# The border between two layers of a one-core trunk: norm loads, last scatter, first key projection and row sums in another order

## The chip, the cores and the metric

The kernel runs on one core of a Trainium2 chip. The time is that of one execution on the device, in microseconds (us). Next to it stands one profiled execution, whose span is somewhat shorter than its time. PE is the matrix engine, PEld its weight load, DVE the vector engine, ACT the scalar engine, POOL the general engine. SP is a queue of its own that only issues DMA transfers here, and POOL issues some too. PEclk is the clock that the matrix engine was granted, as a share of the full one.

## The reference, cut to what matters

Two layers are run one after the other on 512 tokens of width 1024. Each has three parts, and after each part stands a layer norm.

```
for l in range(DEPTH):                                   # DEPTH = 2
    q, k, v, r, a_low, u, v_sgu = split_proj(x @ w_in[l])
    h = concat([gla_group(...), sgu_group(...)]) @ w_out[l]
    x = layer_norm(DN_ALPHA * x + h, ln_g[l, 0], ln_b[l, 0])
    h = mem_xattn(x, mem, wq_x[l], wk_x[l], wv_x[l], wo_x[l])   # keys: mem @ wk_x[l]
    x = layer_norm(DN_ALPHA * x + h, ln_g[l, 1], ln_b[l, 1])
    h = grouped_moe(x, ...)                              # 16 experts, two for each token
    x = layer_norm(DN_ALPHA * x + h, ln_g[l, 2], ln_b[l, 2])
```

The border is the end of the experts of layer 0, the third layer norm of layer 0, the keys of layer 1, which hang on `mem` alone, and the first token projection of layer 1, which needs the normed x.

## The kernel before, in words

Each product of two fp32 matrices is made of three fp16 products: both operands are split into a high and a low half (`mm3`, L168 to L170: high by high, high by low, low by high). The four tiles of 128 tokens are called 0 to 3, and `xr[t]` holds the residual of tile t.

Weights come in units of 1 MB. `feed.fill` (L98) issues their loads on SP as slots come free. `feed.pump` (L124 and L129) splits the next unit that has been loaded: ACT makes `whi` from `raw`, then DVE makes `wlo` from both. `feed.limit` bounds how far the loads may run ahead of the layer. The units of layer 1 begin with wk0 to wk3 (the keys), then k, v0, v1, s0 (the token projections).

The order of the instructions on each engine is the order of the code. Each engine works its own list in order, so an instruction that waits holds up all that stand behind it on that engine.

At the end of the experts, `down(e)` multiplies by the last weight of an expert, ACT writes the result into `rows` (L1234), and POOL issues an indirect scatter of these rows into a table `y` in memory (L1143). `down(14)` is called in the loop, `down(15)` after it. Then every engine reads a counter `cnti` (L1260) and takes a branch (L1261) around an overflow loop, which isn't entered with these inputs. After it the third layer norm, class `LN3`, reads two rows of `y` for each token, `ya` (L399) and `yb` (L400), in tile order on SP's queue. `ya + yb` is made by DVE for tile 0 (L409) and by POOL for tiles 1 to 3 (L405). `a(t)` adds the residual (DVE L412) and takes the variance (ACT L415 to L417). `b(t)` scales by `lng` and `lnb` (DVE L422 and L423).

Around it stands the first stage of layer 1: four `k_proj`, each 48 matmuls on a wk unit and a split of the result into `kT` (ACT L173, DVE L174); `xTr(t)`, eight PE transposes of the normed tile (L310), evicted as `xT` by the same two lines; and `tok_proj(t)`, the first products of layer 1 on `xT`. `warm(10)` (L185) is ten matmuls whose result nobody reads. Much later in layer 1 the output projection splits its own weight units with the same lines L124 and L129.

Of the kernel before, what the change touches and what calls it, by code (L numbers as in the profile page):

```python
# [11 lines left out]
F32 = mybir.dt.float32  # L12
I32 = mybir.dt.int32
AF = mybir.ActivationFunctionType
OP = mybir.AluOpType
# [5 lines left out]
DEPTH = 2  # L21
D = 1024
S = 512
NT = 4
P = 128
KT = 8
NE = 16
# [11 lines left out]
YEND = 4  # L39
# [5 lines left out]
def trunk_kernel(ctx, tc, units, xT, x, memT, alow, wa2, b_a, gn_g, w_sT, b_s, slnT,  # L45
# [12 lines left out]
    def nm(s):  # L58
        cnt[0] += 1
        return f"{s}_{cnt[0]}"  # L60
# [167 lines left out]
    U = []  # L228
# [117 lines left out]
    def kv_open():  # L346
        KV["cm"] = tc.tile_pool(name=nm("kv"), bufs=1, reuse_waits="tile")
        kp = KV["cm"].__enter__()
        KV["k"] = [kp.tile([P, KT, 256], F16, name=nm("kT")) for _ in range(2)]
# [44 lines left out]
    class LN3:  # L394
        def __init__(self, ya, yb):
            ln_exp()
            self.ya, self.yb, self.st = ya, yb, {}
            for t in range(NT):
                nc.sync.dma_start(ya[:, t], y2[t * P:(t + 1) * P, :])  # L399
                nc.sync.dma_start(yb[:, t], y2[S + t * P:S + (t + 1) * P, :])  # L400
                if t == 1:
                    feed.limit = 1 << 30
                    feed.fill()
            for t in range(1, NT):
                pool.tensor_tensor(ya[:, t], ya[:, t], yb[:, t], op=OP.add)  # L405

        def a(self, t):
            if t == 0:
                dve.tensor_tensor(self.ya[:, 0], self.ya[:, 0], self.yb[:, 0], op=OP.add)  # L409
            pre = xr[t]  # L410
            mv_ = lnp[0].tile([P, 6], F32, tag="lnmv", bufs=2, name=nm("lnmv"))
            dve.scalar_tensor_tensor(pre, xr[t], ALPHA, self.ya[:, t], op0=OP.mult, op1=OP.add,  # L412
                                     accum_out=mv_[:, 0:1])
            dve.tensor_scalar(mv_[:, 1:2], mv_[:, 0:1], -1.0 / D, None, op0=OP.mult)
            act.activation(self.yb[:, t], pre, AF.Square, bias=mv_[:, 1:2], accum_out=mv_[:, 2:3])  # L415
            act.activation(mv_[:, 3:4], mv_[:, 2:3], AF.Ln, bias=c_lneps, scale=1.0 / D)
            act.activation(mv_[:, 4:5], mv_[:, 3:4], AF.Exp, scale=-0.5)  # L417
            self.st[t] = pre, mv_

        def b(self, t):  # L420
            pre, mv_ = self.st.pop(t)
            dve.scalar_tensor_tensor(pre, pre, mv_[:, 1:2], lgt["g"], op0=OP.add, op1=OP.mult)  # L422
            dve.scalar_tensor_tensor(xr[t], pre, mv_[:, 4:5], lgt["b"], op0=OP.mult, op1=OP.add)  # L423

    kv_open()
    ln_open()
    for l in range(DEPTH):
        u = U[l]

        with ExitStack() as ex:  # L430
# [25 lines left out]
            if l > 0:  # L456
                k_proj(u, 0)
                third.a(0)
                k_proj(u, 1, 0)
                third.a(1)  # L460
                third.b(0)
                feed.pump(1)
                k_proj(u, 2, 0)
                k_proj(u, 3, 0)
                xTr(0)
                feed.pump(2)
            kg = mp.tile([P, 2, NT, 256], F32, tag="kgu", name="kg")
# [28 lines left out]
            for t in range(NT):  # L496
                if t == NT - 1:
# [3 lines left out]
                    act.activation(al[:, :, 1, 0:16], araw, AF.Copy, scale=SW)  # L501
                if l > 0 and t + 1 < NT:
                    if t + 2 < NT:
                        third.a(t + 2)
                    third.b(t + 1)
                if l > 0 and t == 1:
                    warm(10)
                p = pk[t] if l == 0 else tok_proj(t, [u["k"]], 256)
# [360 lines left out]
        with ExitStack() as ex:  # L869
# [6 lines left out]
            feed.xend = {"h": u["end"], "x": u["end"] - (8 if fin else 0), "y": u["end"] - (8 if fin else YEND), "mem": u["end"]}  # L876
            feed.limit = u["end"] + 4
            feed.rawfree.extend("x" * RAW_X)
# [327 lines left out]

            def down_mm(e, after=None):
                hh, hl = E[e]["hT"]
                pp = []
                for hf in range(2):  # L1210
# [8 lines left out]
                    else:  # L1219
                        feed.pump()  # L1220
                        wh, wl = feed.get(n)
# [7 lines left out]

            def down(e, after=None):  # L1230
                o = rows[:, 2 + e % 2]
                pp = down_mm(e, after)
                for hf in range(2):
                    act.activation(o[:CAP, hf * 512:(hf + 1) * 512], pp[hf][:CAP, :], AF.Copy,  # L1234
                                   scale=(gallw if whole(e, 4 + hf) else gall)[:CAP, e:e + 1])
                scatter(o, idxR[:CAP, e:e + 1])
                del E[e]
# [91 lines left out]
            for e in range(NE - 1 if fin else NE):  # L1329
                gate_up(e)  # L1330
                if e + 1 < NE:
                    dispatch(e + 1)
                hid(e)

# [16 lines left out]

            feed.need(u["end"] - YEND - 1)
            px2c.__exit__(None, None, None)
            if not fin:
                ln_open()
                load_ln(l, 2)
                down(NE - 1)
                pxc.__exit__(None, None, None)
                phc.__exit__(None, None, None)
                with tc.tile_pool(name=f"ovf{l}", bufs=1, reuse_waits="tile") as fp:  # L1360
                    overflow(fp)
            else:

                pxc.__exit__(None, None, None)
                ln_open()
# [100 lines left out]

        if l + 1 < DEPTH:
            kv_open()


# [59 lines left out]
```

## Time and profile before

| | |
|---|---|
| median of 3 runs | 1277.48 us (1275.62 to 1279.99) |
| profiled execution | 1278.14 us, its span 1276.5 us |
| granted clock over the span | 0.972 |
| busy share of the span | PE 92%, DVE 71%, ACT 56%, POOL 18% |

Times in the rows are counted from the start of the span. "Idle before" is the time for which the engine stood still ahead of an instruction, and the name behind the arrow is what ended it. The border lies at about 610 to 690 us.

### The profile page before, as it was taken

Reading aid. Unit: us, or ns where it says so; the run is one execution under the profiler, and the core shown is the slowest. Engines: PE = TensorE matmul, PEld = TensorE weight load, DVE = VectorE, ACT = ScalarE, POOL = GpSimd, SP = SyncE. Lnnn points to the kernel's source line nnn. Section 1 sums busy time; section 2 is a strip of 40 time slices with the busy share of each in tenths; the row PEclk is TensorE's granted clock in tenths of the full one; section 3 lists DMA queues with packets and bytes.
Section 4 is the critical chain, followed back from the end, with each engine's and each line's share of the span. In section 5 each row is a group of like instructions: output and inputs, shape, how many; then the busy total and the mean of one; then the engine's idle time right before and its main releaser. Section 6 shows DMA issues by size and latency. Waiting matters only on the chain. (4 is left out here: it accounts for less than half of the span.)

```text
span 1276.5 us, 26079 instructions
## 1 busy us (share of the span) xinstructions
PE 1172.9 (92%) x11218; PEld 760.2 (60%) x11219; DVE 909.9 (71%) x1066; ACT 711.1 (56%) x810; POOL 234.5 (18%) x193
## 2 busy tenths in 40 slices
PE   7999999999979999999859999999999899999973
PEld 4455456454557777777635545444644777777751
DVE  3255875378579999999474275673857789999977
ACT  3435334345448888888443444232633588888863
POOL 3002000000231223321250003000003222223214
PEclk9999999999989999999979999999998899999996
DMA  9412225227569999999671230154374799999964
GB/s 361 163 67 99 99 77 188 99 99 292 220 226 371 419 418 418 419 417 405 233 273 79 99 133 34 67 215 181 112 312 139 274 389 419 417 419 419 373 241 180
DMA packets 54941, 314.76 MB, mean 247 GB/s; under 512 B 9310, under 2 KB 9406, under 8 KB 22561
## 3 DMA queue, kind: packets, MB, share of 16 engines
q1 hardware_dynamic: 42096, 279.99, 56.0%
q0 software_dynamic: 11568, 28.83, 6.3%
q10 hardware_dynamic: 1152, 4.19, 0.8%
q8 instruction: 90, 1.47, 0.5%
q14 instruction: 35, 0.28, 0.1%
HBM read 302.80 MB, written 22.68 MB: 255 GB/s over the span
## 5 line engine op out<-in xcount | busy, mean ns | idle before, releaser
L129 DVE SCALAR_TENSOR_TENSOR wlo<-raw,whi 128x2048 f16<-128x2048 f32 (+1 forms) x234 | 521.8, 2277 | 101.0 <-ACT whi L124 100.6
L124 ACT ACTIVATE whi<-raw 128x2048 f16<-128x2048 f32 (+1 forms) x239 | 440.9, 1894 | 32.9 <-DMA raw<-in_units 16.7
L170 PE MATMUL ps<-xgh,wlo 128*128 128x96 f16 x2048 | 270.4, 207 | 12.9 <-DVE wlo L129 12.9
L168 PE MATMUL ps<-xgh,whi 128*128 128x96 f16 x2048 | 270.3, 207 | 4.7 <-ACTq L1261 4.2
L169 PE MATMUL ps<-xgl,whi 128*128 128x96 f16 x2048 | 270.2, 207 | 1.1 <-DVE xgl L174 1.1
L170 PEld LDWEIGHTS <-wlo 128*128 128x128 f16 x2400 | 236.4, 98 | 50.7 <-DVE wlo L129 16.7
L168 PEld LDWEIGHTS <-whi 128*128 128x128 f16 x2400 | 236.5, 99 | 39.1 <-issue 6.0
L169 PEld LDWEIGHTS <-whi 128*128 128x128 f16 x2400 | 236.4, 99 | 38.2 <-issue 8.5
L1143 POOL DMA_INDIRECT y<-rows,idxR x31 | 71.4, 2303 | 340.8 <-ACT rows L1234 331.1
L168 PE MATMUL ps<-whi,xT 128*128 128x512 f16 (+1 forms) x256 | 92.6, 362 | 8.4 <-ACT whi L124 7.1
L170 PE MATMUL ps<-whi,xT 128*128 128x512 f16 (+1 forms) x256 | 92.4, 361 | 2.2 <-DVE xT L174 2.2
L169 PE MATMUL ps<-wlo,xT 128*128 128x512 f16 (+1 forms) x256 | 92.5, 361 | 1.7 <-DVE wlo L129 1.7
L168 PE MATMUL ps<-whi,hhl 128*96 128x512 f16 x200 | 75.9, 379 | 1.1 <-ACT hhl L1203 1.1
L169 PE MATMUL ps<-wlo,hhl 128*96 128x512 f16 x200 | 75.7, 379 | 0.9 <-DVE wlo L129 0.9
L170 PE MATMUL ps<-whi,hhl 128*96 128x512 f16 x200 | 75.8, 379 | 0.0
L294 ACT ACTIVATE lnmv<-lnmv,c_lneps 128x1 f32<-128x1 f32 x16 | 4.7, 295 | 110.0 <-DVE lnmv L293 110.0
L1203 ACT ACTIVATE hhl<-h 128x384 f16<-128x384 f32 x32 | 16.7, 523 | 74.9 <-DVE h L1178 74.8
L1216 PE MATMUL ps<-raw,h 128*96 128x512 f32 x112 | 50.3, 592 | 0.0
L169 PE MATMUL ps<-x2T,whi 128*128 128x512 f16 x128 | 48.5, 379 | 1.0 <-DVE x2T L174 1.0
L169 PE MATMUL ps<-wlo,mx 128*128 128x512 f16 x128 | 48.5, 379 | 0.4 <-DVE wlo L129 0.3
L1137 POOL DMA_INDIRECT rows<-xd,idxT x22 | 40.4, 1838 | 45.6 <-DVE wlo L129 11.1
L168 PE MATMUL ps<-x2T,whi 128*128 128x512 f16 x128 | 48.5, 379 | 0.0
(309 smaller groups left out, 2052.2 us busy)
## 6 DMA issues: line engine op xcount, KB each, us to landing
raw<-in_units SPq DMA_DIRECT2D x249, 1024.0 KB
xd<-xr ACTq DMA_DIRECT2D x8, 512.0 KB
ya<-y SPq DMA_DIRECT2D x8, 512.0 KB
yb<-y SPq DMA_DIRECT2D x8, 512.0 KB
y<-zr SPq DMA_DIRECT2D x1, 4096.0 KB
lng<-in_ln_g POOLq DMA_DIRECT2D x6, 512.0 KB, 5.3
lnb<-in_ln_b POOLq DMA_DIRECT2D x6, 512.0 KB, 7.1
raw<-in_xT SPq DMA_DIRECT2D x4, 512.0 KB
```

The source lines that it names most:

```text
L124: act.activation(dest[0], t[:, :cols], AF.Copy, scale=scale)
L129: dve.scalar_tensor_tensor(dest[1], t[:, :cols], scale, dest[0], op0=OP.mult, op1=OP.subtract)
L168: pe.matmul(o, lh, rh, start=first, stop=False)
L169: pe.matmul(o, lh, rl, start=False, stop=False)
L170: pe.matmul(o, ll, rh, start=False, stop=last)
L294: act.activation(mvt[:, 2:3], mvt[:, 1:2], AF.Ln, bias=c_lneps, scale=(ISC * ISC if scaled else 1.0))
L1137: pool.indirect_dma_start(out=dst[:idx.shape[0], :], out_offset=None, in_=xd[:], in_offset=bass.IndirectOffsetOnAxis(ap=idx, axis=0), boun ...
L1143: i = pool.indirect_dma_start(out=y2[:], out_offset=bass.IndirectOffsetOnAxis(ap=idx, axis=0), in_=src[:CAP, :], in_offset=None, bounds_ch ...
L1203: act.activation(f2(hh), h32, AF.Copy)
L1216: pe.matmul(p[:CAP, :], E[e]["h"][:, f * CAP:(f + 1) * CAP], mv(w, f), start=(f == 0), stop=(f == 3))
```

## The change

The norm parameters `lng` and `lnb` of the third norm are loaded while the last expert is still in work, and stand in POOL's queue ahead of the last two scatters. `down(15)` splits no weights, so that ACT writes the rows of expert 15 right behind those of expert 14, and the splits of wk2 and wk3 come after. The keys' first projection stands ahead of the branch. One more unit (k) may be loaded ahead. POOL adds no rows any more: DVE makes all four sums, tile by tile, and POOL only copies one element of `yb[:, 1]`, which keeps the instructions behind it in its list until that tile has landed. The splits, projections and norm steps of the border are written in another order, with one split fewer ahead of `tok_proj(0)` and without `warm(10)`.

```diff
     def kv_open():
-        KV["cm"] = tc.tile_pool(name=nm("kv"), bufs=1, reuse_waits="tile")
+        KV["cm"] = tc.tile_pool(name=nm("kv"), bufs=1, side="right", reuse_waits="tile")
...
-            for t in range(1, NT):
-                pool.tensor_tensor(ya[:, t], ya[:, t], yb[:, t], op=OP.add)
+
+            w = lnp[0].tile([P, 1], F32, tag="lnst", bufs=2, name=nm("lnst"))
+            pool.tensor_copy(w, yb[:, 1, 0:1])
+
+        def add(self, t):
+            dve.tensor_tensor(self.ya[:, t], self.ya[:, t], self.yb[:, t], op=OP.add)
 
         def a(self, t):
-            if t == 0:
-                dve.tensor_tensor(self.ya[:, 0], self.ya[:, 0], self.yb[:, 0], op=OP.add)
...
             if l > 0:
-                k_proj(u, 0)
+                feed.pump(1)
+                k_proj(u, 1, 0)
+                third.add(0)
                 third.a(0)
-                k_proj(u, 1, 0)
-                third.a(1)
+                third.add(1)
                 third.b(0)
                 feed.pump(1)
+                third.a(1)
                 k_proj(u, 2, 0)
+                feed.pump(1)
                 k_proj(u, 3, 0)
                 xTr(0)
-                feed.pump(2)
+                third.b(1)
...
-                if l > 0 and t + 1 < NT:
-                    if t + 2 < NT:
-                        third.a(t + 2)
+                if l > 0 and 0 < t < NT - 1:
                     third.b(t + 1)
-                if l > 0 and t == 1:
-                    warm(10)
+                if l > 0 and t + 2 < NT:
+                    third.add(t + 2)
+                    third.a(t + 2)
...
-            feed.limit = u["end"] + 4
+            feed.limit = u["end"] + 5
...
-            def down_mm(e, after=None):
+            def down_mm(e, after=None, pump=1):
...
-                        feed.pump()
+                        feed.pump(pump)
...
                 if e + 1 < NE:
                     dispatch(e + 1)
+                else:
+
+                    px2c.__exit__(None, None, None)
+                    ln_open()
+                    load_ln(l, 2)
                 hid(e)
...
-            feed.need(u["end"] - YEND - 1)
-            px2c.__exit__(None, None, None)
             if not fin:
-                ln_open()
-                load_ln(l, 2)
-                down(NE - 1)
+                down(NE - 1, None, 0)
                 pxc.__exit__(None, None, None)
                 phc.__exit__(None, None, None)
+                feed.pump(2)
+
+                kv_open()
+                k_proj(U[l + 1], 0, 0)
                 with tc.tile_pool(name=f"ovf{l}", bufs=1, reuse_waits="tile") as fp:
                     overflow(fp)
```

ACT's list at the end of the experts, before: `rows` with gall are the rows of expert 14 (first pair) and 15 (second pair), and the two splits between them are wk2 and wk3.

```order
L1234 ACTIVATE rows_2934<-ps_7507,gall 96x512
L1234 ACTIVATE rows_2934<-ps_7524,gall 96x512
L124 ACTIVATE whi_7565<-raw_7282 128x2048
L124 ACTIVATE whi_7582<-raw_7294 128x2048
L1234 ACTIVATE rows_2934<-ps_7564,gall 96x512
L1234 ACTIVATE rows_2934<-ps_7581,gall 96x512
L1260 TENSOR_LOAD cnti
L1261 COMPARE_AND_BRANCH
```

The same place of the change:

```order
L1238 ACTIVATE rows_2934<-ps_7515,gall 96x512
L1238 ACTIVATE rows_2934<-ps_7534,gall 96x512
L1238 ACTIVATE rows_2934<-ps_7566,gall 96x512
L1238 ACTIVATE rows_2934<-ps_7579,gall 96x512
L124 ACTIVATE whi_7599<-raw_7282 128x2048
L124 ACTIVATE whi_7603<-raw_7294 128x2048
L173 ACTIVATE kT_7610<-ps_7612 128x512
L1264 TENSOR_LOAD cnti
L1265 COMPARE_AND_BRANCH
```

The rows of expert 15 moved ahead of both splits, and the first keys' eviction (kT) ahead of the branch.

DVE's list behind the branch, before, up to the eviction of the first transposed tile: xr_85 is tile 0, xr_86 tile 1, raw_7809 is unit k, raw_7811 is v0.

```order
L129 SCALAR_TENSOR_TENSOR wlo_7877<-raw_7809,whi_7876 128x2048
L409 TENSOR_TENSOR ya<-ya,yb 128x1024
L412 SCALAR_TENSOR_TENSOR xr_85,lnmv_7883<-xr_85,ya 128x1024
L174 SCALAR_TENSOR_TENSOR kT_7798<-ps_7889,kT_7797 128x512
L412 SCALAR_TENSOR_TENSOR xr_86,lnmv_7940<-xr_86,ya 128x1024
L422 SCALAR_TENSOR_TENSOR xr_85<-xr_85,lnmv_7883,lng_7560 128x1024
...
L129 SCALAR_TENSOR_TENSOR wlo_7949<-raw_7811,whi_7948 128x2048
...
L174 SCALAR_TENSOR_TENSOR xT_7824<-ps_8056,xT_7824 128x4x128
```

The same place of the change, where raw_7520 is unit k, raw_7862 v0 and raw_7864 v1:

```order
L129 SCALAR_TENSOR_TENSOR wlo_7876<-raw_7520,whi_7875 128x2048
...
L409 TENSOR_TENSOR ya<-ya,yb 128x1024
L414 SCALAR_TENSOR_TENSOR xr_85,lnmv_7933<-xr_85,ya 128x1024
...
L424 SCALAR_TENSOR_TENSOR xr_85<-xr_85,lnmv_7933,lng_7504 128x1024
L425 SCALAR_TENSOR_TENSOR xr_85<-xr_85,lnmv_7933,lnb_7506 128x1024
L129 SCALAR_TENSOR_TENSOR wlo_7943<-raw_7862,whi_7942 128x2048
L414 SCALAR_TENSOR_TENSOR xr_86,lnmv_7948<-xr_86,ya 128x1024
L416 TENSOR_SCALAR lnmv_7948<-lnmv_7948 128x1
L174 SCALAR_TENSOR_TENSOR kT_7611<-ps_7954,kT_7610 128x512
L129 SCALAR_TENSOR_TENSOR wlo_8006<-raw_7864,whi_8005 128x2048
L174 SCALAR_TENSOR_TENSOR kT_7611<-ps_8011,kT_7610 128x512
L174 SCALAR_TENSOR_TENSOR xT_7874<-ps_8062,xT_7874 128x4x128
```

The norm of tile 0 now stands ahead of the split of v0, and two splits (v0 and v1) with the first step of tile 1's norm between them stand ahead of the eviction of the transposed tile.

POOL's list of the change around the branch, with the rows of the loop left out; before, the norm parameters stood between the last two scatters, and three sums in the place of the copy.

```order
L279 DMA lng_7504<-in_ln_g 128x1024
L279 DMA lnb_7506<-in_ln_b 128x1024
L1147 DMA y_93<-rows_2934,idxR 1024x1024 x2
L1264 TENSOR_LOAD cnti
...
L406 COPY lnst_7872<-yb 128x1
...
L500 DMA araw<-in_alow 128x128
...
L528 DMA bsb<-in_b_s 128x512
L528 DMA gnb<-in_gn_g 128x512
...
L535 DMA wst<-in_w_sT 128x512
```

Both loads moved ahead of the scatter pair, and what POOL loads for layer 1 (bsb, gnb, wst, 256 KB each) now waits for one copy in place of three sums.

## Rows read from the trace of the kernel before

**Rows 1.** Page, costliest groups: busy and mean ns of one, idle before.

```profile
L129 DVE SCALAR_TENSOR_TENSOR wlo<-raw,whi 128x2048 f16<-128x2048 f32 (+1 forms) x234 | 521.8, 2277 | 101.0 <-ACT whi L124 100.6
```

**Rows 2.** Windows: stretch, length, busy of the engines, clock, DMA share, GB/s.

```profile
612.00:620.00 8.00, 3.66 (x17) 1.73 (x15) 7.97 (x7) 8.00 (x7) 3.34 (x3) 1.00 0.19 75
...
630.00:640.00 10.00, 10.00 (x94) 8.98 (x92) 0.00 (x0) 0.00 (x0) 1.94 (x1) 1.00 1.01 402
...
658.00:672.00 14.00, 12.48 (x62) 7.81 (x63) 12.66 (x12) 7.21 (x10) 6.88 (x15) 0.72 0.75 243
```

**Rows 3.** Timeline of PE: start, duration, what it does, idle before.

```profile
621.22 0.27 PE L168 MATMUL ps<-mhl,whi 128*128 128x256 f16 x1 [4.67 <-ACTq L1261]
...
643.73 0.27 PE L170 MATMUL ps<-mhl,wlo 128*128 128x256 f16 x1
657.99 1.94 PE L310 MATMUL ps<-ident,xr 128*128 128x128 f32 x8 [13.99 <-DVE xr L423]
...
661.90 0.39 PE L170 MATMUL ps<-whi,xT 128*128 128x256 f16 x1 [1.52 <-DVE xT L174]
...
665.07 0.42 PE L170 MATMUL ps<-whi,xT 128*128 128x256 f16 x1
665.28 0.42 PE L168 MATMUL ps<-whi,xT 128*128 128x256 f16 x1
...
672.26 2.32 PE L185 MATMUL ps<-ones 128*128 128x512 f16 x10
```

**Rows 4.** Timeline of ACT.

```profile
619.88 1.24 ACT L1234 ACTIVATE rows<-ps,gall 96x512 f32<-96x512 f32 x2
...
640.22 1.91 ACT L124 ACTIVATE whi<-raw 128x2048 f16<-128x2048 f32 x1 [11.25 <-DMA raw<-in_units]
...
648.73 0.20 ACT L417 ACTIVATE lnmv<-lnmv 128x1 f32<-128x1 f32 x1
```

**Rows 5.** Timeline of DVE.

```profile
644.37 1.22 DVE L409 TENSOR_TENSOR ya<-ya,yb 128x1024 f32<-128x1024 f32 x1
645.62 1.23 DVE L412 SCALAR_TENSOR_TENSOR xr<-xr,ya 128x1024 f32<-128x1024 f32 x1
...
654.60 3.25 DVE L423 SCALAR_TENSOR_TENSOR xr<-xr,lnmv,lnb 128x1024 f32<-128x1024 f32 x1
...
657.77 2.28 DVE L129 SCALAR_TENSOR_TENSOR wlo<-raw,whi 128x2048 f16<-128x2048 f32 x1
...
661.17 1.27 DVE L174 SCALAR_TENSOR_TENSOR xT<-ps,xT 128x512 f16<-128x512 f32 x2
...
669.45 1.28 DVE L423 SCALAR_TENSOR_TENSOR xr<-xr,lnmv,lnb 128x1024 f32<-128x1024 f32 x1
```

**Rows 6.** Timeline of POOL.

```profile
616.65 2.49 POOL L1143 DMA_INDIRECT y<-rows,idxR  x1 [14.01 <-ACT rows L1234]
...
621.41 2.55 POOL L1143 DMA_INDIRECT y<-rows,idxR  x1 [1.08 <-ACTq L1261]
...
650.34 6.43 POOL L405 TENSOR_TENSOR ya<-ya,yb 128x1024 f32<-128x1024 f32 x2 [9.93 <-DMA yb<-y]
...
658.14 2.06 POOL L487 TENSOR_SCALAR_AFFINE_SELECT tri<-tri 128x128 f32<-128x128 f32 x1
```

**Rows 7.** Timeline of SP's queue: when its transfers were issued.

```profile
628.56 0.34 SPq L399 DMA_DIRECT2D ya<-y  x1
...
633.50 0.33 SPq L400 DMA_DIRECT2D yb<-y  x1
...
637.65 0.32 SPq L400 DMA_DIRECT2D yb<-y  x1
```

**Rows 8.** DMA issues of 616 to 618 us, then of 590 to 700: median us to landing.

```profile
y<-rows,idxR POOLq DMA_INDIRECT x1, 5.3
...
y<-rows,idxR POOLq DMA_INDIRECT x3, 7.0
```

**Rows 9.** Timeline of ACT in layer 1's output projection.

```profile
796.94 3.70 ACT L124 ACTIVATE whi<-raw 128x2048 f16<-128x2048 f32 x2
```

More of the change, by code (lines that the diff above doesn't have):

```diff
@@ L1228, in down_mm, with down @@
                 return pp
-            def down(e, after=None):
+            def down(e, after=None, pump=1):
                 o = rows[:, 2 + e % 2]
-                pp = down_mm(e, after)
+                pp = down_mm(e, after, pump)
                 for hf in range(2):
@@ L1332, in trunk_kernel @@
                     dispatch(e + 1)
+                else:
+                    px2c.__exit__(None, None, None)
+                    ln_open()
+                    load_ln(l, 2)
                 hid(e)
@@ L1350, in trunk_kernel @@
             dve.tensor_copy(cnti, cntf)
-            feed.need(u["end"] - YEND - 1)
-            px2c.__exit__(None, None, None)
             if not fin:
-                ln_open()
-                load_ln(l, 2)
-                down(NE - 1)
+                down(NE - 1, None, 0)
                 pxc.__exit__(None, None, None)
                 phc.__exit__(None, None, None)
+                feed.pump(2)
+                kv_open()
+                k_proj(U[l + 1], 0, 0)
                 with tc.tile_pool(name=f"ovf{l}", bufs=1, reuse_waits="tile") as fp:
@@ L1362, in trunk_kernel @@
             else:
+                feed.need(u["end"] - YEND - 1)
+                px2c.__exit__(None, None, None)
                 pxc.__exit__(None, None, None)
@@ L1465, in trunk_kernel @@
                 ln_close()
-        if l + 1 < DEPTH:
-            kv_open()
 def pack(i):
```

## Prediction

> **What bounds the kernel now.** I read the page's costliest groups first, then the windows, then the timeline of each engine over the border. Over the whole span the matrix engine is the busy one, but at the border it is not: it stands still for 4.67 us behind the last expert, runs the four key projections without a gap, and then stands still for 13.99 us until the normed first tile is there; 1.52 us more go by before the low half of the transposed tile [rows 3]. These 20.2 us are what the change can touch. The reader should follow them back from the first transpose.
>
> The transposes at 657.99 wait for `b(0)`, whose last instruction starts on DVE at 654.60 and takes 3.25 us [rows 5]. `a(0)` starts with its sum at 644.37, although the rows of `y` for tile 0 were there by 633.5: the `yb` load of tile 2, issued then, had waited for that of tile 0 to land, and the last one, at 637.65, for that of tile 1 [rows 7]. Between lies the split of unit k, which DVE has ahead of the sum and which ACT begins at 640.22 after 11.25 us of waiting for the load of k [rows 4]. That load stands behind four row loads, so it lands 11.7 us after the first of these is issued at 628.56 [rows 7]. And the row loads wait for the scatter of expert 15, issued at 621.41 after ACT's branch [rows 6], because ACT wrote its rows only at 619.88, behind two splits [rows 4], and it lands 7.0 us after its issue, the median of three, of which the middle one took 5.3 [rows 8]. So the chain is: rows of expert 15, scatter, row loads, load of k, split of k, norm of tile 0, transposes.
>
> **The change, part by part.**
>
> *Rows ahead of splits, norm parameters ahead of both scatters.* The last matmul of expert 15 ends at 621.22 - 4.67 = 616.55 [rows 3]. ACT then writes expert 15's rows at once: two by 0.62 us [rows 4], done at 617.6 or so. POOL is still busy with the scatter of expert 14, 616.65 + 2.49 = 619.14 [rows 6], and issues the last scatter there instead of at 621.41: 2.3 us sooner. Its landing is bounded by 5.3 us with nothing ahead of it and by 7.0 us as before [rows 8]: 624.4 to 626.1. I take 5.3, because the 1 MB of norm parameters no longer lies ahead of it; the high end goes into the range.
>
> *First keys and two splits ahead of the branch.* PE runs the first projection in the place of the 4.67 us of idling: 192 matmuls took from 621.22 to 643.73 [rows 3], 0.118 each on the mean, 48 of them less than 5.7 us, and without the slow start 5.2. It ends near 621.8. DVE halves wk2 and wk3 by 617.6 + 1.9 + 2 x 2.28 = 624.1 [rows 1, 4] and evicts the first keys by 0.64, as two take 1.27 [rows 5], so it passes the branch at about 624.8. The row loads wait for this and for the scatter; the first is issued at T = 624.9 in place of 628.56, 3.7 us sooner. PE waits about 3 us at the branch for DVE before the second projection, and three of them and the transposes end at 624.9 + 3 x 5.25 + 1.0 = 641.7. This wait costs nothing, since the next thing that PE needs comes later still.
>
> *One more unit loaded ahead, sums on DVE.* k is loaded before the row loads, its split no longer stands ahead of tile 0's norm. Rows of tile 0 are there at T + 4.9 = 629.8, of tile 1 at T + 9.1 = 634.0 [rows 7]. DVE makes two sums of 1.22, two steps of 1.4, and `b(0)` in 2 x 1.28, the price of these lines without POOL's sums beside them (3.25 with them) [rows 5]. POOL needs 3.2 for one sum, 6.43 for two [rows 6], so the sums are cheaper on DVE: 4.9 us for four of them, of which two lie in the shadow of the loads. `b(0)` ends at about 638.2, so the transposes run as soon as PE is through at 640.7.
>
> *The stall that takes its place.* In ACT's and DVE's lists the eviction of the transposed tile stands behind the split of v0, `a(1)` and the split of v1. v0 now has the place that k had in the queue and lands at T + 11.7 = 636.6. From there: ACT 1.9 to 638.5, DVE 2.3 to 640.8 [rows 1, 4], `a(1)` with ACT's square, log and exp 3.3 to 644.1 (645.62 to 648.93 in the rows of tile 0 [rows 4, 5]), one key eviction 0.6, v1's high half 1.9 to 646.6, its low half 2.3 to 648.9, the low halves of the last keys and of the first transposed block 0.64 each: 650.2. The third matmul of `tok_proj(0)`, the first that needs the low half, stood at 661.90 [rows 3]. It moves by -11.7 us. PE idles for some 8 us before it, in place of 14 and 1.5.
>
> *Clock.* Before, the stretch from 658 to 672 had a granted clock of 0.72, part at 1.2 and part at 2.4 GHz [rows 2], and matmuls at a pitch of 0.21 us up to 665.28, where the keys have a mean of 0.118, their slow start included [rows 3]; the engine had stood idle ahead of it. It again stands idle ahead of the same matmuls, so I take the same cost: zero net, and 2 us (some 20 matmuls by 0.10) if the clock stays up.
>
> *`warm(10)` gone.* The ten matmuls take 2.32 us of PE, 2.2 to the next one [rows 3]. Without them `tok_proj(1)` meets the eviction of its tile, at most 0.64 + 0.64 [rows 5] less the two matmuls that need only the high half; I take 0.8. Net -1.4, bounds -2.2 and 0.
>
> *One split fewer ahead.* Three splits in place of four stand in the border. The unit is then split later, and the feed stays one behind until a stage makes it good. In the output projection ACT does two splits in 3.70 us [rows 9]; a third there is worth from 0 (hidden) to 2.3 us (DVE's half exposed). I take +1.0, as PE has matmuls of the other half in that time.
>
> *Left at zero.* The norm parameters are loaded earlier, beside the last weights ahead of the border; uncovered they would delay these by 1 MB at 402 GB/s, 2.5 us. What covers them: from 612 to 620 the transfers took only 0.19 of their engines [rows 2], so the weights had landed well before their splits, and wk2 and wk3 are split 1.4 us later now. The pool's other side moves only addresses. DVE's 4.9 us of sums lie in its waits; in the stretch from 658 to 672 it is busy for 12.66 of 14 us [rows 2], and two sums there, 2.4 us, would cost as much if nothing else moved away. But the two splits of 660 to 665 have moved ahead.
>
> **Sum.** -11.7 - 1.4 + 1.0 = -12.1 us. On the profiled execution 1278.14 - 12.1 = 1266.0; this execution is 0.7 above the median, so 1265.5 on the median's footing.
>
> A rule speaks against part of this. The Trainium skill, GPSIMD Engine Reference, section 8 (Key points), says that POOL shares its memory interfaces with DVE, with contention in DVE instructions of two SBUF inputs. The trace agrees for POOL's sums (3.25 against 1.28). What POOL does behind its one-element copy, fills and a mask, now falls at 634 to 642, beside `b(0)`. In the trace POOL's 2.06 us mask at 658.14 [rows 6] lies beside a DVE split that took 2.28 [rows 5], which is the mean [rows 1]. So I take no slowing, and leave the other case as a rival.
>
> **Rivals.** (0.3% of the time, 3.8 us, is about what a measurement of this kernel can tell from no change.)
> - *Late landing, 0.20.* The last scatter lands no sooner than before after its issue, or something else holds the row loads: T between 626.3 and 628.56. The chain behind is rigid, so the gain shrinks by 1.4 to 3.7 us: 1267 to 1269.5.
> - *POOL's fills slow DVE, 0.06.* `b(0)` at 3.2 + 3.2 ends at 642 in place of 638.2, and the low half of v0 with all that follows is 3.5 us later: 1269. For it: the 3.25 row. Against it: the 2.28 row.
> - *The clock stays up and the split is hidden, 0.17.* -2 and -1: 1262.5. For it: the idle stretch is 8 us, not 14. Against it: the matmuls behind 13.99 us of idling were slow, and no row shows that 8 us are short enough.
> - *A new wait on SP, slower, 0.03.* v0, v1 and s0 are issued between the row loads of tiles 1 and 2. If one of them waits for a slot that only the split of v0 gives free, the rows of tiles 2 and 3 come after 640 and DVE meets them behind its other work. It is slower than before only if tile 2's sum comes more than 16 us late. I find the slots of wk1 to wk3 free by 624, so little speaks for it: 1282.
> - *Given back later, 0.04.* Layer 1's loads are a stream of their own; if they keep their dates the experts of layer 1 wait for them and the whole is within 0.3%: 1276. Against it: loads are issued as splits free slots, so they move with the border.
>
> The forecast itself has 0.50; its own range, from the landing (0 to +1.4), `warm` (-0.8 to +1.4) and the lost split (-1 to +1.3), is 1263 to 1268. The 80% range takes in the fast rival and the two late ones: 1261 to 1270.5. Faster by over 0.3%: 0.50 + 0.20 + 0.06 + 0.17 = 0.93; within: 0.04; slower: 0.03.
>
> **What would show it.** Right: the last scatter near 619.1, the first row load near 625, the first projection without a gap behind the last expert, a PE wait of 3 us at the branch, transposes near 641, then a wait of about 8 us until 650 ended by DVE's low half, the two instructions of each `b(t)` at 1.3 us. Wrong: transposes later than 645, a row load later than 626.5, `tok_proj(0)` at full pitch from its first matmul, or an idle PE of more than 2 us in layer 1 where there was none.

## The result, and the profile after

The changed kernel takes 1268.47 us (median of 5 runs, 1266.62 to 1269.43) where the kernel before, in the same comparison, takes 1277.48. The ratio is 0.9924 with a 95% interval of 0.9913 to 0.9936, a gain of 9.7 us with 8.2 to 11.1 as its bounds. Forecast were 12.1 us of gain and 1265.5 us, in a range of 1261 to 1270.5. The measured time lies in that range, 0.5 us above the narrower one that the forecast gave for its own mechanism (1263 to 1268).

The profiled execution has a span of 1266.7 us, 9.8 less than before. Its border begins 0.8 us later on the clock of the trace, which comes from an input load in the first 15 us (ACT waits 5.02 us for it, before 3.12) and has nothing to do with the change: ACT's first instruction on the last expert's `hhl` starts at 610.13, before at 609.31. So lengths are better read from this instruction on. From it to the transposes of the last tile the border took 82.57 us before (to 691.88) and takes 70.92 now (to 681.05): 11.65 us less. Both ends and the transposes of the tiles between, in the timelines of ACT and PE before:

```profile
609.31 0.52 ACT L1203 ACTIVATE hhl<-h 128x384 f16<-128x384 f32 x1 [3.26 <-DVE h L1178]
```

```profile
671.39 1.04 PE L310 MATMUL ps<-ident,xr 128*128 128x128 f32 x8
...
682.22 1.04 PE L310 MATMUL ps<-ident,xr 128*128 128x128 f32 x8
...
691.88 1.04 PE L310 MATMUL ps<-ident,xr 128*128 128x128 f32 x8
```

The timeline of PE after, with the idle time before each row, beside [rows 3]:

```profile
625.48 0.27 PE L168 MATMUL ps<-mhl,whi 128*128 128x256 f16 x1 [2.87 <-DVEq L1265]
...
628.67 0.42 PE L170 MATMUL ps<-mhl,wlo 128*128 128x256 f16 x1
628.88 0.42 PE L168 MATMUL ps<-mhl,whi 128*128 128x256 f16 x1
...
642.86 1.04 PE L310 MATMUL ps<-ident,xr 128*128 128x128 f32 x8
649.25 0.40 PE L168 MATMUL ps<-whi,xT 128*128 128x256 f16 x1 [5.36 <-ACT xT L173]
...
651.80 0.39 PE L170 MATMUL ps<-whi,xT 128*128 128x256 f16 x1 [1.94 <-DVE xT L174]
...
656.04 0.42 PE L169 MATMUL ps<-wlo,xT 128*128 128x256 f16 x1
656.26 0.42 PE L170 MATMUL ps<-whi,xT 128*128 128x256 f16 x1
...
661.73 1.04 PE L310 MATMUL ps<-ident,xr 128*128 128x128 f32 x8
...
671.39 1.04 PE L310 MATMUL ps<-ident,xr 128*128 128x128 f32 x8
...
681.05 1.04 PE L310 MATMUL ps<-ident,xr 128*128 128x128 f32 x8
```

The 20.2 us of idling have become 10.2: 2.87 at the branch, 5.36 and 1.94 ahead of `tok_proj(0)`. The transposes no longer wait for `b(0)`. The third matmul of `tok_proj(0)` moved from 661.90 to 651.80, and still runs at the slow pitch of 0.21 us. Behind the branch, too, PE runs at this pitch, from 625.9 to 629.3; the granted clock from 626 to 630 is 0.58.

The timeline of ACT after, beside [rows 4]:

```profile
610.13 0.52 ACT L1207 ACTIVATE hhl<-h 128x384 f16<-128x384 f32 x1 [3.25 <-DVE h L1182]
...
615.96 2.39 ACT L1238 ACTIVATE rows<-ps,gall 96x512 f32<-96x512 f32 x4
...
638.42 1.91 ACT L124 ACTIVATE whi<-raw 128x2048 f16<-128x2048 f32 x1
644.14 1.15 ACT L417 ACTIVATE yb<-xr,lnmv 128x1024 f32<-128x1024 f32 x1 [3.80 <-DVE lnmv L416]
...
646.32 1.90 ACT L124 ACTIVATE whi<-raw 128x2048 f16<-128x2048 f32 x1
...
648.60 1.09 ACT L173 ACTIVATE xT<-ps 128x512 f16<-128x512 f32 x2
```

The timeline of DVE after, beside [rows 5]:

```profile
633.82 1.22 DVE L409 TENSOR_TENSOR ya<-ya,yb 128x1024 f32<-128x1024 f32 x1
...
639.23 1.28 DVE L425 SCALAR_TENSOR_TENSOR xr<-xr,lnmv,lnb 128x1024 f32<-128x1024 f32 x1
640.43 2.28 DVE L129 SCALAR_TENSOR_TENSOR wlo<-raw,whi 128x2048 f16<-128x2048 f32 x1
...
648.26 2.29 DVE L129 SCALAR_TENSOR_TENSOR wlo<-raw,whi 128x2048 f16<-128x2048 f32 x1 [1.11 <-ACT whi L124]
650.47 0.68 DVE L174 SCALAR_TENSOR_TENSOR kT<-ps,kT 128x512 f16<-128x512 f32 x1
651.07 1.28 DVE L174 SCALAR_TENSOR_TENSOR xT<-ps,xT 128x512 f16<-128x512 f32 x2
```

Read the two together from the bottom: the low half of the transposed tile comes at 651.07 because DVE makes v1's low half first; that waits for ACT's high half at 646.32, which stands behind the square of tile 1 at 644.14, which waits for DVE's first norm step behind v0's low half at 640.43. This is the stall that the forecast had in the place of the old ones.

The timelines of POOL and of SP's queue, and the DMA issues of 616 to 625 us (count, median us to landing), beside [rows 6 to 8]:

```profile
617.49 2.53 POOL L1147 DMA_INDIRECT y<-rows,idxR  x1 [12.84 <-ACT rows L1238]
620.32 2.97 POOL L1147 DMA_INDIRECT y<-rows,idxR  x1 [0.30 <-ACT whi L124]
635.96 0.38 POOL L406 COPY lnst<-yb 128x1 f32<-128x1 f32 x1 [12.68 <-DMA yb<-y]
...
638.67 0.59 POOL L500 DMA_DIRECT2D araw<-in_alow  x1
```

```profile
626.37 0.34 SPq L399 DMA_DIRECT2D ya<-y  x1
```

```profile
y<-rows,idxR POOLq DMA_INDIRECT x2, 5.8
```

In layer 1's output projection PE now waits for a weight split, beside [rows 9]:

```profile
792.62 0.38 PE L169 MATMUL ps<-wlo,mx 128*128 128x512 f16 x1 [1.79 <-DVE wlo L129]
798.22 0.38 PE L169 MATMUL ps<-wlo,mx 128*128 128x512 f16 x1 [0.26 <-DVE wlo L129]
```

From the last transposes at the border to the first logarithm of the norm behind this stage (ACT L294) it is 811.54 - 691.88 = 119.66 us before and 802.49 - 681.05 = 121.44 after: 1.8 us of the border's 11.65 are given back here. The two logarithms in the timelines of ACT, before and after:

```profile
811.54 0.29 ACT L294 ACTIVATE lnmv<-lnmv,c_lneps 128x1 f32<-128x1 f32 x1 [8.63 <-DVE lnmv L293]
```

```profile
802.49 0.29 ACT L294 ACTIVATE lnmv<-lnmv,c_lneps 128x1 f32<-128x1 f32 x1 [6.85 <-DVE lnmv L293]
```

### The profile page after: what moved, and what is told of

Read it like the earlier page. It is cut to its first block, busy times and chain, and to the rows that moved or that the text cites. A ratio compares the mean times of both kernels' runs of the same rounds, so it can differ in the third digit from the quotient of the medians.

```text
span 1266.7 us, 26049 instructions
## 1 busy us (share of the span) xinstructions
PE 1170.5 (92%) x11208; PEld 760.3 (60%) x11209; DVE 907.4 (72%) x1069; ACT 711.5 (56%) x810; POOL 225.1 (18%) x191
## 5 line engine op out<-in xcount | busy, mean ns | idle before, releaser
L170 PE MATMUL ps<-xgh,wlo 128*128 128x96 f16 x2048 | 271.7, 208 | 13.1 <-DVE wlo L129 12.6
L168 PEld LDWEIGHTS <-whi 128*128 128x128 f16 x2400 | 237.1, 99 | 39.8 <-issue 10.6
L294 ACT ACTIVATE lnmv<-lnmv,c_lneps 128x1 f32<-128x1 f32 x16 | 4.7, 295 | 108.3 <-DVE lnmv L293 108.3
```

Source lines behind the costliest of these rows:

```text
L168: pe.matmul(o, lh, rh, start=first, stop=False)
L170: pe.matmul(o, ll, rh, start=False, stop=last)
L294: act.activation(mvt[:, 2:3], mvt[:, 1:2], AF.Ln, bias=c_lneps, scale=(ISC * ISC if scaled else 1.0))
```

## The experiments

Each is the changed kernel with one edit, unless it says otherwise; the prices of the single edits do not add up to the whole, as each edit is taken out with all others in place. Ratios are to the kernel before, measured beside it; the changed kernel has 0.9924. "Border" is the length from the last `hhl` to the last tile's transposes, as above. T is the start of the first row load, and "third matmul" that of the third matmul of `tok_proj(0)`, both counted from the same `hhl`.

| kernel | ratio (95%) | T | third matmul | border | against the changed kernel |
|---|---|---|---|---|---|
| before | 1 | 19.25 | 52.59 | 82.57 | +11.65 |
| changed | 0.9924 (0.9913 to 0.9936) | 16.24 | 41.67 | 70.92 | |
| e1 sums on POOL | 0.9930 (0.9905 to 0.9954) | 16.25 | 43.82 | 73.15 | +2.2 |
| e2 rows late | 0.9927 (0.9902 to 0.9953) | 17.48 | 43.71 | 73.20 | +2.3 |
| e3 keys behind | 0.9919 (0.9897 to 0.9942) | 16.40 | 43.49 | 73.14 | +2.2 |
| e4 limit 4 | 0.9987 (0.9973 to 1.0001) | 16.29 | 50.67 | 79.40 | +8.5 |
| e5 evict first | 0.9901 (0.9884 to 0.9918) | 16.32 | 36.16 | 70.47 | -0.5 |
| e6 warm back | 0.9934 (0.9920 to 0.9948) | 16.20 | 42.55 | 72.75 | +1.8 |
| e7 fourth split | 0.9913 (0.9897 to 0.9928) | 16.34 | 42.71 | 71.76 | +0.8 |
| e8 clock fill | 0.9898 (0.9881 to 0.9915) | 16.35 | 41.68 | 68.59 | -2.3 |
| e9 norm between | 0.9936 (0.9921 to 0.9951) | 20.50 | 44.81 | 73.60 | +2.7 |
| e10 tile late | 0.9841 (0.9827 to 0.9855) | 16.31 | 36.07 | 64.66 | -6.3 |
| e11 with split | 0.9885 (0.9869 to 0.9901) | 16.34 | 36.16 | 69.47 | -1.5 |
| e12 sum first | 0.9906 (0.9889 to 0.9923) | 16.23 | 42.92 | 71.11 | +0.2 |

The time intervals, about 2 us to either side, tell only e4, e10 and e11 apart from the changed kernel; for the others the lengths in one trace each are what there is. These have a spread of their own: in e6 and e7 nothing ahead of the load of v0 makes it later, and the third matmul is 0.9 and 1.0 us later than in the changed kernel, 0.0 in e8. So a difference of 1 us at the third matmul is not read by itself.

What lies behind is more regular. Where the order of the lists is that of the changed kernel, the third matmul stands 11.4 us behind the start of v0's low half on DVE, in nine traces to 0.01 us (13.3 in e1). That low half starts once `b(0)` on DVE and v0's high half on ACT are both done. In the changed kernel they end at 640.51 and 640.33, within 0.2 us; `b(0)` is the last also in e1, e3, e4, e8 and e12, the high half, after a wait for the load of v0, in e2, e6, e7 and e9.

**e1, sums on POOL.**

```diff
-            pool.tensor_copy(w, yb[:, 1, 0:1])
+            for t in range(1, NT):
+                pool.tensor_tensor(ya[:, t], ya[:, t], yb[:, t], op=OP.add)
...
-            dve.tensor_tensor(self.ya[:, t], self.ya[:, t], self.yb[:, t], op=OP.add)
+            if t == 0:
+                dve.tensor_tensor(self.ya[:, t], self.ya[:, t], self.yb[:, t], op=OP.add)
```

> The changed kernel with the sums of tiles 1 to 3 on POOL again (tile 0 stays on DVE, the order of everything else stays). Theory (the sums on DVE are cheap because DVE's two b(0) instructions no longer run beside POOL's sums): b(0) goes back to about 3.2 us an instruction and ends near 644 in place of 640.5, the split of v0 and all behind it moves with it, and the third matmul of tok_proj(0) stands near 655 in place of 651.8: about 3.5 us slower than the changed kernel, 1272 us. Rival (which engine adds doesn't matter here, the chain of loads and splits does): b(0) at 1.3 us each, the time within 1 us of 1268.5.

The third matmul is 2.2 us later. The place is another than expected: `b(0)` hardly suffers (1.82 and 1.28, 0.2 us at the start of v0's low half), but the split of v1, on the chain, does. POOL's sums of tiles 2 and 3 and the split on DVE, from the two timelines:

```profile
645.90 4.82 POOL L406 TENSOR_TENSOR ya<-ya,yb 128x1024 f32<-128x1024 f32 x2 [7.48 <-DMA yb<-y]
```

```profile
648.62 4.25 DVE L129 SCALAR_TENSOR_TENSOR wlo<-raw,whi 128x2048 f16<-128x2048 f32 x1 [1.10 <-ACT whi L124]
```

The split takes 4.25 us in place of 2.29; its first 2.1 us lie beside the sums, the rest beside POOL's fills, as far as POOL's ends can be trusted. So 1.96 of the 2.2 us are this one instruction. The theory that sums on POOL slow DVE holds; it had named `b(0)` and put the price at 3.5 us. The Trainium skill, GPSIMD Engine Reference, section 8 (Key points), says that POOL shares its memory interfaces with DVE and disturbs DVE instructions with two SBUF inputs; this split has two, and the trace agrees. In the changed kernel POOL's fills at 636 to 639 lie beside `b(0)`, which keeps its 1.28.

**e2, rows of expert 15 behind the splits.**

```diff
-                down(NE - 1, None, 0)
+                down(NE - 1)
...
-                feed.pump(2)
```

> The changed kernel with the splits of wk2 and wk3 inside down(15) again, so that ACT writes the rows of expert 15 behind them. Theory (rows, scatter, row loads, load of v0 are one rigid chain): the last scatter is issued near 622 in place of 620.3, the first row load near 628.2 in place of 626.4, and everything to tok_proj(0) moves by about 1.8 us: 1270.3 us. Rival (the row loads wait for DVE at the branch, so the scatter's place is hidden): first row load unmoved, 1268.5 us.

The last scatter is issued 2.4 us later, but the row loads start 4.9 us behind it in place of 6.0, so T is only 1.2 us later. The third matmul is 2.0 us later. What goes beyond T is the load of v0, which lands 12.9 us after T, where it was there after 12.1 at most. The chain holds, as the theory said, the size to within what a trace tells.

**e3, first keys behind the branch.**

```diff
-                kv_open()
-                k_proj(U[l + 1], 0, 0)
                 with tc.tile_pool(name=f"ovf{l}", bufs=1, reuse_waits="tile") as fp:
                     overflow(fp)
+                kv_open()
+                k_proj(U[l + 1], 0, 0)
```

> The changed kernel with the first key projection behind the branch again. Theory (PE is not what the border waits for, its 5.4 us of idling ahead of tok_proj(0) take up the 5.3 us): the transposes stand near 648 in place of 642.9, the third matmul of tok_proj(0) within 1 us of 651.8, the time 1268.5 to 1270 us. Rival (the first projection in PE's idle time is a gain in itself): the whole is some 5 us slower, 1273.5 us.

The transposes stand 34.4 us behind `hhl` in place of 32.7, the third matmul 1.8 us later: between the two. PE's idling took up most of the projection, as the theory had it; what was missed is that ACT has the first keys' eviction in its list ahead of the split of k, so that this split came 20.8 us behind `hhl` instead of 15.0 and pushed DVE's list: the sum of tile 0 starts 1.8 us later. The ratio tells nothing either way.

**e4, the old bound on loads.**

```diff
-            feed.limit = u["end"] + 5
+            feed.limit = u["end"] + 4
```

> The changed kernel with the old bound on loads, so that unit k is loaded behind the first four row loads again; its split still stands first in DVE's list. Theory (k's load ahead of the row loads is the greatest single part): k lands some 10 us after the first row load, near 636.5, its low half ends near 641 in place of 629.3, the sums and b(0) follow, and the third matmul of tok_proj(0) stands near 658.5 in place of 651.8: 7 us slower, 1275.5 us. Rival (v0's load is the gate, and it lands at the same place or little later): the time within 2.6 us (one more unit of 1 MB) of 1268.5.

This one is clear in the time, too: 0.9987, a gain over before of next to nothing. DVE's split of k in its timeline:

```profile
639.10 2.29 DVE L129 SCALAR_TENSOR_TENSOR wlo<-raw,whi 128x2048 f16<-128x2048 f32 x1 [14.73 <-ACT whi L124]
```

DVE stands still for 14.73 us behind the branch, with the rows of tile 0 there for more than half of it, if they take the 4.9 us from T that they took before. The one unit loaded ahead is the greatest single part of the change, 8.5 us at the border; without it all other edits together are worth 3.2 there. What it would give alone to the kernel before was not tried.

**e5, evictions ahead of two splits.**

```diff
                 third.add(1)
                 third.b(0)
-                feed.pump(1)
                 third.a(1)
                 k_proj(u, 2, 0)
-                feed.pump(1)
                 k_proj(u, 3, 0)
                 xTr(0)
+                feed.pump(2)
                 third.b(1)
```

> The changed kernel with the splits of v0 and v1 behind the transposes of tile 0, so that the eviction of the transposed tile stands ahead of them in ACT's and DVE's lists. Theory (the new stall of PE ahead of tok_proj(0) comes from these two splits standing first): the third matmul of tok_proj(0) stands near 645.5 in place of 651.8; the v0 and v1 halves are then made while PE does the 24 matmuls of k, with up to 2 us of waiting for them: 4 to 6 us faster than the changed kernel, 1263.5 us. Rival (the splits are needed as soon as the evictions, so their order moves the wait from the first matmuls to those of v0): the same wait of 5 to 7 us ahead of the matmuls of v0, time within 1.5 us of 1268.5.

The theory was right at tile 0, and nearly the whole gain went at tile 1. The timeline of PE, then that of ACT:

```profile
646.99 0.28 PE L170 MATMUL ps<-whi,xT 128*128 128x256 f16 x1 [0.56 <-DVE xT L174]
...
655.61 1.04 PE L310 MATMUL ps<-ident,xr 128*128 128x128 f32 x8
661.04 0.40 PE L168 MATMUL ps<-whi,xT 128*128 128x256 f16 x1 [4.39 <-ACT xT L173]
```

```profile
657.94 1.15 ACT L417 ACTIVATE yb<-xr,lnmv 128x1024 f32<-128x1024 f32 x1 [7.87 <-DVE lnmv L416]
...
660.39 1.08 ACT L173 ACTIVATE xT<-ps 128x512 f16<-128x512 f32 x2
```

`tok_proj(0)` started 5.5 us sooner. But in ACT's list the square of tile 2 stands ahead of the eviction of tile 1, and it waited 7.87 us for DVE, which was at the two splits, `b(1)` and then the sum and first step of tile 2. Neither theory nor rival had named this place.

**e10, then, puts the norm step of the next tiles behind the transposes.** It is e5 with

```diff
-                if l > 0 and t + 2 < NT:
-                    third.add(t + 2)
-                    third.a(t + 2)
                 p = pk[t] if l == 0 else tok_proj(t, [u["k"]], 256)
...
                 if l > 0 and t + 1 < NT:
                     xTr(t + 1)
+                if l > 0 and t + 2 < NT:
+                    third.add(t + 2)
+                    third.a(t + 2)
```

> The kernel e5 (splits of v0 and v1 behind the eviction of tile 0) with the sum and first norm step of tiles 2 and 3 behind the transposes of the tile before. Theory (in e5 the gain of 5 us at tile 0 was lost at tile 1, since ACT's square of tile 2 stands ahead of the eviction of tile 1 and waits for DVE, 4.4 us on PE, with a stretch at the low clock behind it): the wait at tile 1 falls under 1 us, the gain of tile 0 stays: 4.5 to 6 us faster than the changed kernel, 1263 us. Rival (DVE is full in this stretch, so that any order only moves the wait): a wait of over 2 us at tile 1 or 2, within 1.5 us of e5's 1266.8 us.

```profile
645.00 0.28 PE L170 MATMUL ps<-whi,xT 128*128 128x256 f16 x1 [0.56 <-DVE xT L174]
654.27 1.04 PE L310 MATMUL ps<-ident,xr 128*128 128x128 f32 x8
655.61 0.28 PE L168 MATMUL ps<-whi,xT 128*128 128x256 f16 x1 [0.30 <-ACT xT L173]
656.34 0.28 PE L170 MATMUL ps<-whi,xT 128*128 128x256 f16 x1 [0.34 <-DVE xT L174]
```

The timeline of PE shows 0.64 us of waiting at tile 1 in place of 4.39, and the time is 1259.3 us, 0.9841 of before. This version beats both kernels. Its border is 6.3 us shorter than the changed kernel's, and its profiled execution 6.5 us; the ratios differ by 0.0083, 10.6 us. Of the 4 us between, 2.7 come from this, that its profiled execution, at 1261.97, was the slowest of its five; the rest is less than the intervals tell.

**e11, e10 with a fourth split** (`if l > 0 and t == 0: feed.pump(1)` behind the norm step of tile 2).

> The kernel e10 with the fourth split (s0) behind the first norm step of tile 2. Theory (the fourth split is worth 2.4 us in the output projection and hides at the border): 2 to 2.5 us faster than e10, 1260.5 us. Rival (it delays DVE's norm of tile 2 and comes back as a wait at the transposes of tile 2): the same as e10.

```profile
669.19 1.06 PE L310 MATMUL ps<-ident,xr 128*128 128x128 f32 x8 [3.99 <-DVE xr L425]
```

A miss: the timeline of PE has a wait of 3.99 us at tile 2, for `b(2)`, because ACT and DVE have the split of s0 ahead of it there. That is the rival's mechanism at a higher price, since the time is 5.3 us above e10's. The fourth split does shorten the stretch behind the border, to 119.66 us in place of e10's 121.42. Behind `b(2)` might be the place; this was not tried.

**e6, `warm(10)` back**, ahead of `tok_proj(1)` as before.

> The changed kernel with warm(10) ahead of tok_proj(1) again. Theory (the ten matmuls cost their 2.2 us less the wait for the eviction of tile 1 that they covered): 0.7 to 1.4 us slower, 1269.5 us. Rival (they kept the clock up or covered the whole wait): same time within 0.3 us, or faster.

The ten matmuls stand behind the transposes of tile 1. From these to those of tile 2 it is 10.83 us here and before (682.22 - 671.39), and 9.66 us in the changed kernel (671.39 - 661.73) and in the eight other variants that have the same order here without them. So the ten matmuls cost 1.2 us, as the theory had it. The rest of the 1.8 lies ahead of them: the load of v0 is 1.0 us later. The time (0.9934) fits and proves nothing.

**e7, a fourth split at the border.**

```diff
                 xTr(0)
+                feed.pump(1)
                 third.b(1)
```

> The changed kernel with a fourth split (s0) at the border, behind the transposes of tile 0. Theory (with three splits the feed stays one behind, and pays in the output projection with PE waits of 2.1 us): those waits go, and the border loses nothing that PE waits for, or up to 1 us as DVE's list grows by 2.3 us ahead of b(1): 1 to 2 us faster than the changed kernel, 1267 us. Rival (the output projection's waits have another cause, or the split delays tile 1): the same time or slower by 2 us.

The border is no shorter, but the output projection takes 799.49 - 680.43 = 119.06 us in place of 121.44, and its waits for a split are gone. Between third matmul and last transposes the split costs nothing (29.05 against 29.25). So, against e7, one split fewer costs 2.4 us later on. The time, 0.9913, leans that way inside its interval.

**e8, thirty matmuls that nobody reads** (`warm(30)` between the transposes of tile 0 and `tok_proj(0)`).

> The changed kernel with 30 matmuls that nobody reads (some 6.5 us) between the transposes of tile 0 and tok_proj(0). Theory (PE idles there and its clock is granted at half afterwards): the matmuls of tok_proj(0) then run at 0.11 us each from the first, 20 to 22 of them 0.10 us faster: 2 us faster than the changed kernel, 1266.5 us. Rival (the clock falls for another reason, or the low-clock matmuls hide behind a later wait): tok_proj(0) slow as before or a wait in its place, same time or slower.

The timeline of PE:

```profile
645.37 6.64 PE L185 MATMUL ps<-ones 128*128 128x512 f16 x30
...
653.44 0.28 PE L170 MATMUL ps<-whi,xT 128*128 128x256 f16 x1 [1.21 <-DVE xT L174]
653.56 0.27 PE L168 MATMUL ps<-whi,xT 128*128 128x256 f16 x1
653.66 0.27 PE L169 MATMUL ps<-wlo,xT 128*128 128x256 f16 x1
```

The matmuls run at a pitch of 0.11 us, and the border is 2.3 us shorter. The windows of the same 18 us, first of the changed kernel and then of this one, show the granted clock in the third column from the end, 0.72 and 1.00:

```profile
642.00:660.00 18.00, 10.70 (x58) 6.63 (x56) 11.79 (x15) 7.50 (x14) 1.41 (x4) 0.72 0.84 332
```

```profile
644.00:662.00 18.00, 16.79 (x101) 9.71 (x98) 11.43 (x15) 8.27 (x16) 1.04 (x4) 1.00 0.81 321
```

**e9, the norm parameters between the last two scatters**, as before, with all else of the change.

> The changed kernel with the norm parameters loaded between the last two scatters again (the rows of expert 15 still right behind those of expert 14). Theory (1 MB of norm parameters ahead of the last scatter holds it up by some 2 us, in POOL's issue by 1.2 and in landing): the last scatter is issued near 621.5 in place of 620.3 and the first row load near 628.2 in place of 626.4, the whole 1.5 to 2 us slower than the changed kernel, 1270 us. Rival (the landing of the scatter is the same and DVE's branch or the list of DVE behind the first row load takes up the rest): less than 0.7 us.

The last scatter is issued 11.3 us behind `hhl` (620.53 - 609.21), in the changed kernel 10.2, so 1.1 us later; the DMA issues of 616 to 625 us show the landing of the last two:

```profile
y<-rows,idxR POOLq DMA_INDIRECT x2, 8.8
```

8.8 us in place of 5.8, T later by 4.3, the third matmul by 3.1. The theory holds in kind, at more than twice its price for T (1.8 us): 3.0 of the 4.3 us are the landing. Before, with the same 1 MB ahead of it, the last scatter took less, 7.0 us by the median of three [rows 8].

**e12, the first norm step ahead of the second keys.**

```diff
-                k_proj(u, 1, 0)
                 third.add(0)
                 third.a(0)
+                k_proj(u, 1, 0)
                 third.add(1)
```

> The changed kernel with the sum and first norm step of tile 0 ahead of the second key projection in the lists. Theory (the norm of tile 0 was late by 2 us because DVE has the eviction of the second keys ahead of it, and these came late as PE ran at the low clock behind its wait at the branch): the sum starts near 631.5 in place of 633.8, the norm of tile 0 ends near 638.3 in place of 640.5 and the third matmul of tok_proj(0) stands near 650 in place of 651.8: 1.5 to 2 us faster, 1266.7 us. Rival (the load of v0, split from 638.4, is the gate): the sum moves, the split of v0 doesn't, the same time within 0.5 us.

Neither. The sum starts 1.6 us sooner, at 632.27, but the norm of tile 0 does not end sooner. The eviction of the second keys now stands between its first step and `b(0)`, and DVE waits for it. The timeline of DVE:

```profile
637.44 0.69 DVE L174 SCALAR_TENSOR_TENSOR kT<-ps,kT 128x512 f16<-128x512 f32 x1 [2.48 <-ACT kT L173]
...
641.70 2.28 DVE L129 SCALAR_TENSOR_TENSOR wlo<-raw,whi 128x2048 f16<-128x2048 f32 x1
```

v0's low half starts behind `b(0)`, 31.6 us behind `hhl` where it was 30.3, and the third matmul is later by the same 1.25 us. The edit did not bring the norm forward, so it cannot tell whether an earlier norm would have helped. The load of v0 was not the last here, although it landed late. The timeline of ACT:

```profile
638.83 1.91 ACT L124 ACTIVATE whi<-raw 128x2048 f16<-128x2048 f32 x1 [1.43 <-DMA raw<-in_units]
```

It lands 12.5 us after T here, 13.0 and 13.1 in e6 and e7, at most 12.1 in the changed kernel (638.42 - 626.37) and at most 11.7 in e1.

## Why the prediction was right, point by point

**Bottleneck and chain: right.** Rows of expert 15, scatter, row loads, then unit loads and their splits are one chain. e2, e9 and e4 each break one link of it, and the third matmul moves by 2.0, 3.1 and 9.0 us.

**The stall that takes its place: right in kind and place.** The forecast had transposes at 640.7, then PE idle until about 650 for DVE's low half, behind v0, `a(1)` and v1. Measured are 642.86 and 651.80, by the same rows, on a clock on which the border begins 0.8 us later. e5 shows that the order of the splits makes this stall.

**Its size: 0.8 us too good.** The -11.7 us of the sum are -10.9 on a clock that starts at the last `hhl` (52.59 to 41.67). The loss lies ahead of v0's low half, which starts 30.3 us behind `hhl` where 29.2 was forecast; from there on the forecast took 11.7 us and it is 11.4. Two steps were too good, and both end here within 0.2 us of each other.
- T was put at 3.7 us sooner and is 3.0 (19.25 to 16.24): the scatter took 5.8 us to land where I took 5.3, and POOL stood still for 0.3 us ahead of it. The high bound for its landing, 7.0, was kept for the range.
- The second keys were put at full pitch, "without the slow start". PE ran 16 of these matmuls at 0.21 us (625.9 to 629.3), some 1.7 us in all. DVE evicts these keys ahead of the sum of tile 0, and `b(0)` ended at 640.51, on the forecast's clock 639.7 where 638.2 was forecast.

As `b(0)` is the later of the two and DVE runs without a pause of over 0.21 us from the sum to its end, a scatter that landed as forecast would have gained next to nothing by itself. An earlier `b(0)` would have gained 0.2 us with ACT's high half where it was. Whether that would have come sooner, too, stays open: it stands in ACT's list behind the same norm, and how early the load of v0 landed is not known.

**`warm(10)`: -1.4 forecast, -1.2 measured** (10.83 to 9.66 between the transposes of tiles 1 and 2, and e6).

**One split fewer: +1.0 forecast, +1.8 measured** against before, 2.4 against e7, at the upper bound of 2.3. The error was to let PE's other matmuls hide half of it: in this trace PE had none left to do, and waited 1.79 and 0.26 us for DVE's low halves. The length is sure, its makeup less so. From the last transposes to the logarithm it is 121.3 to 121.4 us in all eleven traces with three splits, 119.1 to 119.7 in the three with four (before, e7, e11). But in e6, e8 and e12 PE waits for no split there: from 100 to 120 us behind the last transposes the granted clock is 0.91, where the changed kernel has 1.00, and the length is the same.

**Clock: right in kind, not quite zero.** It again stood at the lower level ahead of and into `tok_proj(0)`, and was worth 2.3 us, as e8 gave back. But the 22 matmuls from the third on all run at the slow pitch, where before 18 did, and from the third matmul to the transposes of tile 1 it is 9.93 us in place of 9.49: +0.4 that the sum had at zero. That it would fall at the branch as well was left out, as said above.

**The parts left at zero** held: DVE's sums show no wait of PE; the last expert's matmuls did not come later by the norm parameters.

**The sum.** On the trace -10.9 + 0.4 - 1.2 + 1.8 = -9.9 us, where -11.7 + 0 - 1.4 + 1.0 = -12.1 was forecast: the terms miss by 0.8, 0.4, 0.2 and 0.8 us, all to the same side. The spans differ by 9.8, as the later start of the border (0.8) and a shorter rest behind the logarithm (0.8) cancel. (From the median before, 1277.48 - 12.1 is 1265.4, not 1265.5.) The time lies where the late rival had it (1267 to 1269.5), but its mechanism did not occur: it asked for a first row load between 626.3 and 628.56, and on the same clock this is at 625.55. That the time fell into the wide range is thus in part luck: it was widened for that rival. POOL's fills did not slow DVE, the clock did not stay up, and nothing was given back in the experts. No new wait on SP held up the norm of tiles 2 and 3.

## What to carry to other kernels

Where engines work their lists in order, look up for each engine on the chain what stands in its list between the arrival of an operand and the instruction that uses it, and put nothing there that waits for something later. After a change of order, follow it for the next tile as well: in e5 five microseconds gained at tile 0 were lost at tile 1 to a square that stood one place too early, and moving it, in e10, shortened the border by 5.8 us against e5 and gave the fastest version. And look first at which load the chain waits for: one unit of 1 MB loaded ahead of the row loads was worth 8.5 us with the other edits in place, more than any other edit of the change. Last, an edit that moves one step forward in a list moves the others back: in e12 the sum came sooner and the norm's end later.

## What the runs showed of the hardware that was not expected

- The first row load, which waits for the last indirect scatter of 96 rows, starts 6.0 to 6.2 us after that scatter's issue in the changed kernel and the ten variants in which that scatter is issued 2.8 us behind the one ahead of it with no loads between. It is 4.9 us in e2, where the two are 5.2 us apart, and 7.2 before and 9.2 in e9, with 1 MB of loads between them.
- The load of 1 MB behind four row loads landed between at most 11.7 us (e1) and 13.1 us (e7) after the first of these in executions in which nothing ahead of it differs.
- A DVE split of 2.29 us took 4.25, about half of it beside POOL sums (e1), while POOL's fills of 0.1 to 0.5 us beside DVE's norm left it at 1.28.
- Thirty matmuls whose result nobody reads, 6.6 us of them in a wait of 7.3, kept the granted clock at 1.00 where it was at 0.72 without them, and this was 2.3 us of the border (e8).
